# S5 input products: fp32 matmuls on four row tiles of 32 in place of split parts stacked by transfers

## The chip, the cores and the metric

One core of one Trainium2 chip runs the whole kernel. TensorE (PE in the profile, PEld its weight loads) multiplies, VectorE (DVE) and ScalarE (ACT) do elementwise work, GpSimd (POOL) some small work, SyncE (SP) issues the transfers. The metric is the device time of one execution in microseconds, as the median of several runs; lower is better.

## The reference

One decoder layer for 256 tokens of width 2048, in float32. After an RMS norm, one large projection (`w_in`) feeds three parallel branches: S5, a state-space scan; an RG-LRU scan; and stick-breaking attention. Each branch goes through its own projection and a sigmoid gate, the sum goes through `w_out`, and a squared-ReLU MLP and a last norm follow. The part that matters here is the start of the S5 branch:

```python
ug = u32.transpose(1, 0, 2).reshape(L, bsz, S5_GROUPS, S5_GROUP)      # 64 groups of 16 channels
bu = lax.complex(jnp.einsum('lbgc,gpc->lbgp', ug, jnp.real(b_bar)),   # 64 states for each group
                 jnp.einsum('lbgc,gpc->lbgp', ug, jnp.imag(b_bar)))
...
h = linear_scan(a, bu)
y = (einsum(real(h), c_re) - einsum(imag(h), c_im)) + d_skip * u32
```

Every group of 16 channels is multiplied by a small matrix B (16 x 64, a real and an imaginary part), which gives 64 complex inputs of a linear scan along the 256 tokens; C brings the scan's states back to 16 channels.

## The kernel before

**Weights.** All large weights stream in units of 256 x 512 (512 KB). For each unit SyncE issues a load into `raw` (three buffers, line 130), ScalarE rounds it to the matmul's reduced fp32 format into `hi` (line 146), VectorE subtracts to get the rest `lo` (line 147; four buffers for each of the two), and TensorE multiplies hi by hi, hi by lo and lo by hi (lines 225 to 227 with 256 columns at a time in `chunk`, 241 to 243 with 512 in `chunk_tok`, 276 to 278 in `pair_tok`). `next_unit` (line 151) keeps loads up to four and splits up to three units ahead of the unit in use.

**Side work.** Everything else is written as Python generators, whose steps end at `yield`. After each unit, `pump` (line 179) lets every running generator advance by its rate of steps per unit, and orders what they issue behind that unit's last instructions. S5 runs at 1.27 steps a unit (`S5_RATE`, line 590). The Tile framework then settles the order on each engine at compile time: it takes instructions by priority, lets one that is not ready be passed by one that is, and puts semaphores between engines and on reused buffers.

**PSUM.** It has two pools of four banks each: `psm` for the large products and `pss` (line 58, tag "ps") for all small ones: S5's input products `ps_v`, its output products `ps_y`, and attention's `ps_z`, `ps_c` and `ps_o`. A bank comes free when the last reader of its tile is done.

**S5.** The 1024 channels lie in eight blocks of 128 (`us5`, 128 x 8 x 256 in fp32). A block has eight groups of 16 channels, that is four pairs; a pair fills 32 partitions and yields 128 states (the partitions of a product), for the real and the imaginary part. Before, a block's input products were made in three stages.
- `s5_split` (lines 618 to 625): ScalarE rounds the block's channels (620), VectorE takes the rest (621); for each of the two groups of a pair ScalarE multiplies B by a mask that zeroes the other group's rows (624), and VectorE takes the rest of that (625). The results lie in `ux`.
- `s5_stack` (lines 629 to 631): for each pair `t` three transfers, issued by SyncE, put the rounded parts and the rests under each other in `stk`, so that 96 partitions hold channels hi, lo, hi against B hi, hi, lo.
- Then `s5_scan` makes, for each pair `t`, two matmuls over these 96 rows (line 654, real and imaginary part, 256 columns each) into one bank `ps_v`, and ScalarE copies the bank into `v` (line 656). A step ends after every second pair.

The split of the next block follows the copies, its transfers are issued during the first four scans. VectorE then turns `v` by the tables (lines 665 to 675), scans (line 710), turns back (lines 686 to 697); eight fp32 matmuls on four column tiles of 32 (line 703, `tile_position=(0, t * 32)`) give the block's output `ps_y`, and VectorE adds the skip term from that bank (line 705). There is no step's end between line 705 of one block and the first input products of the next, so both belong to one step.

S5 runs beside the LRU branch's gates, attention's projections and attention, and its own gates; `finish(sq)` closes it before the `w_glu` products.

Of the kernel before, what the change touches and what calls it, by code (L numbers as in the profile page):

```python
# [9 lines left out]
F32 = mybir.dt.float32  # L10
# [12 lines left out]
NG = 64  # L23
NT = 4
PAR = {"norm_mix_g": 16, "norm_mlp_g": 16, "s5_d": 8, "s5_b_glu": 8, "lru_conv_b": 8,
       "lru_lambda": 8, "lru_b_r": 8, "lru_b_i": 8, "lru_conv_w": 32, "grp_mask": 2, "steps": 16}
DFF = 8192
NH = 8
EPS = 1e-6
# [17 lines left out]
def hybrid_block(ctx: ExitStack, tc: tile.TileContext, io, out):  # L47
# [239 lines left out]
    def small(name):  # L287
        o = 0
        for n_, w_ in PAR.items():
            if n_ == name:  # L290
                return par[:, o:o + w_]
            o += w_
# [12 lines left out]
    s5 = ExitStack()  # L305
    sp = s5.enter_context(tc.tile_pool(name="s5", bufs=1))
    us5 = sp.tile([P, WT, L], F32, name="us5")
    bco = sp.tile([P, WT, 2, 64], F32, name="bco")
    ce = sp.tile([P, 2, 32, 2, 16], F32, name="ce")
    ux = sp.tile([P, 4, L], F32R, name="ux")  # L310
    rad = sp.tile([P, 32], F32, name="rad")
    fw = sp.tile([P, 2, 32], F32, name="fw")
    pp = s5.enter_context(tc.tile_pool(name="s5w", bufs=1))
# [66 lines left out]
    def v2(t):  # L380
        return t.rearrange("p (a l) -> p a l", a=2)
# [4 lines left out]

    dsk = small("s5_d")
    bgl = small("s5_b_glu")
    mask = small("grp_mask")
    steps = small("steps")  # L390

    def repeat(a, n):
# [222 lines left out]
        f = "p n a b -> p n (a b)"  # L615
        return (c.rearrange(f), s.rearrange(f)), gen()

    def s5_split(ct):
        bx = [ux[:, 2 + i, :].rearrange("p (r g s) -> p r g s", r=2, g=2) for i in range(2)]
        nc.scalar.copy(ux[:, 0, :], us5[:, ct, :])  # L620
        nc.vector.tensor_tensor(ux[:, 1, :], us5[:, ct, :], ux[:, 0, :].bitcast(F32), ALU.subtract)
        for g in range(2):
            m = mask[:, g:g + 1]
            nc.scalar.activation(bx[0][:, :, g, :], bco[:, ct], AF.Copy, scale=m)
            nc.vector.scalar_tensor_tensor(bx[1][:, :, g, :], bco[:, ct], m, bx[0][:, :, g, :].bitcast(F32), ALU.mult, ALU.subtract)

    stk = sp.tile([P, NT, 2, L], F32R, tag="stk", name="stk")[0:96]

    def s5_stack(t):
        for i, w_ in enumerate((ux[:, 0:4:2, :], ux[:, 1:3, :], ux[:, 0:4:3, :])):  # L630
            nc.sync.dma_start(stk[i * 32:i * 32 + 32, t].bitcast(F32), w_[t * 32:t * 32 + 32].bitcast(F32))

    gq = []

    def s5_scan():
        v = ypool.tile([P, 2, NT, L], F32, tag="yhi", name="s5_v")
        t12 = ypool.tile([P, 2, NT, L], F32, tag="ylo", name="s5_t")
        vr, vi, t1, t2 = v[:, 0], v[:, 1], t12[:, 0], t12[:, 1]
        tabs, more = s5_tables(0)
        yield from more  # L640
        s5_split(0)
        yield
        yield
        for t in range(NT):
            s5_stack(t)
            yield
        tt = nc.vector.tensor_tensor
        for b in range(WT):
            c, s = tabs
            t3 = pp.tile([P, NT, L], F32, tag="t3", name=f"t3_{b}")  # L650
            for t in range(NT):
                ps = pss.tile([P, CH], F32, tag="ps", name=f"ps_v{b}")
                for i in range(2):
                    nc.tensor.matmul(ps[:, i * L:(i + 1) * L], stk[:, t, 1, i * P:(i + 1) * P], stk[:, t, 0, :], start=i == 0, stop=True,
                                     skip_group_check=True)
                nc.scalar.copy(v[:, :, t, :], v2(ps))
                if t % 2:
                    yield
            more = iter(())
            if b + 1 < WT:  # L660
                s5_split(b + 1)
                tabs, more = s5_tables(b + 1)
                yield
            next(more, None)
            tt(t1, vr, c, ALU.mult)
            yield
            tt(t2, vi, s, ALU.mult)
            yield
            tt(t1, t1, t2, ALU.add)
            yield  # L670
            tt(t3, vi, c, ALU.mult)
            yield
            tt(vr, vr, s, ALU.mult)
            yield
            tt(t3, t3, vr, ALU.subtract)
            next(more, None)
            yield
            for x_ in (t1, t3):
                for t in range(NT):
                    j = b * NT + t  # L680
                    tt_scan(x_[:, t, :], rad[:, j:j + 1].broadcast_to([P, L]), x_[:, t, :])
                    if b + 1 < WT and x_ is t1:
                        s5_stack(t)
                    yield
            next(more, None)
            tt(t2, t1, c, ALU.mult)
            yield
            tt(vr, t3, s, ALU.mult)
            next(more, None)
            yield  # L690
            tt(t2, t2, vr, ALU.subtract)
            yield
            tt(vi, t3, c, ALU.mult)
            yield
            tt(t1, t1, s, ALU.mult)
            yield
            tt(t1, t1, vi, ALU.add)
            yield
            yield
            ps = pss.tile([P, CH], F32, tag="ps", name=f"ps_y{b}")  # L700
            for k, w_ in enumerate((t2, t1)):
                for t in range(NT):
                    nc.tensor.matmul(ps[t * 32:t * 32 + 32, 0:L], ce[:, k, b * NT + t, :, :], w_[:, t, :], start=k == 0, stop=k == 1,
                                     skip_group_check=True, tile_position=(0, t * 32))
            nc.vector.scalar_tensor_tensor(us5[:, b, :], us5[:, b, :], dsk[:, b:b + 1], ps[:, 0:L], ALU.mult, ALU.add)
            if b % 2:
                gq.append(later([gelu(b)], 1.0))
# [403 lines left out]
def _lay_out(inp):  # L1111
    import numpy as np

    def chan(a, n):
        return np.ascontiguousarray(np.asarray(a).reshape(n, P).T)

    def units(a):
        a = np.asarray(a)
        k, n = a.shape
        u = a.reshape(k // (P * UK), UK, P, n // CH, CH).transpose(3, 0, 2, 1, 4)  # L1120
        return np.ascontiguousarray(u).reshape(-1, P, UK, CH)

    o = {}
    x = np.asarray(inp["x"])[0]
    o["x"] = np.ascontiguousarray(x.T.reshape(KT, P, L).transpose(1, 0, 2))
    for n in ("w_in", "w_br_s5", "w_br_lru", "w_br_attn", "w_out", "w_up", "w_down"):
        o[n] = units(inp[n][0])
    o["w_glu"] = units(inp["s5_w_glu"][0])
    o["x_res"] = np.ascontiguousarray(x.reshape(2, P, D).transpose(1, 0, 2))
    o["b_gate_row"] = np.ascontiguousarray(np.asarray(inp["b_gate"][0]).reshape(1, -1))  # L1130
    o["norm_mix_g"] = chan(inp["norm_mix_g"][0], KT)
    o["norm_mlp_g"] = chan(inp["norm_mlp_g"][0], KT)
    o["final_norm_g"] = np.ascontiguousarray(np.asarray(inp["final_norm_g"]).reshape(1, D))
    for n in ("s5_d", "s5_b_glu", "lru_conv_b", "lru_lambda"):
        o[n] = chan(inp[n][0], WT)
    o["lru_b_r"] = chan(np.asarray(inp["lru_b_r"][0]).reshape(-1), WT)
    o["lru_b_i"] = chan(np.asarray(inp["lru_b_i"][0]).reshape(-1), WT)
    o["lru_conv_w"] = np.ascontiguousarray(np.asarray(inp["lru_conv_w"][0]).reshape(4, WT, P).transpose(2, 0, 1))
    for n in ("lru_w_r", "lru_w_i"):
        o[n] = np.ascontiguousarray(np.asarray(inp[n][0]).reshape(WT, 2, 64, 64).transpose(1, 2, 0, 3))  # L1140
    o["s5_lam"] = np.ascontiguousarray(np.stack([np.asarray(inp[n][0]).reshape(32, 2, 64).transpose(1, 2, 0).reshape(P, 32)
                                                 for n in ("s5_lam_re", "s5_lam_im")], axis=1))
    o["s5_log_dt"] = np.ascontiguousarray(np.asarray(inp["s5_log_dt"][0]).reshape(32, 2).T)
    o["s5_b"] = np.ascontiguousarray(np.stack([np.asarray(inp[n][0]).reshape(WT, 8, 64, 16).transpose(1, 3, 0, 2).reshape(P, WT, 64)
                                               for n in ("s5_b_re", "s5_b_im")], axis=2))
    o["s5_c"] = np.ascontiguousarray(np.stack([np.asarray(inp[n][0]).reshape(32, 2, 16, 64).transpose(1, 3, 0, 2).reshape(P, 32, 16)
                                               for n in ("s5_c_re", "s5_c_im")], axis=1))
    m = np.zeros((P, 2), np.float32)
    m[(np.arange(P) // 16) % 2 == 0, 0] = 1.0
    m[(np.arange(P) // 16) % 2 == 1, 1] = 1.0  # L1150
    o["grp_mask"] = m
    o["steps"] = np.tile(np.arange(16, dtype=np.float32), (P, 1))
    o["lru_conv_w"] = o["lru_conv_w"].reshape(P, 4 * WT)
    o["par"] = np.concatenate([o.pop(n) for n in PAR], axis=1)
    return o
# [20 lines left out]
```

## Time and profile before

| | |
|---|---|
| median of 3 runs | 1495.38 us (1493.66 to 1497.81) |
| the profiled execution's span | 1495.0 us |
| mean granted TensorE clock | 0.997 |
| TensorE busy | 1479.8 us (99%) |
| VectorE busy | 1174.3 us (79%) |
| ScalarE busy | 775.5 us (52%) |
| transfers | 292.41 MB, mean 196 GB/s |
| first and last `ps_v` matmul | 133.9 and 540.4 us |

Times in the views are microseconds from the span's start. A row of the timeline has the start, the length, the engine, the line, the operation, what it writes and reads, and the form; "x4" means that four like instructions in a row are merged, from the first one's start to the last one's end. The end of a matmul is modelled and matmuls overlap in the array, so the step from one start to the next tells what a matmul costs the engine, and its length does not. Behind a row, in brackets, stands the idle time of the engine before it and what ended it. Rows of the view of waits have the engine and what waited, what it waited for, the total, the count and the longest. Rows of the view of stretches have the stretch, its length, the busy time and count of each engine (TensorE, weight loads, VectorE, ScalarE, GpSimd), the granted clock, the share of the transfer engines and GB/s.

### The profile page before, as it was taken

What the parts mean: (1) busy time and instruction counts of PE and PEld (TensorE: products, weight loads), DVE (VectorE), ACT (ScalarE), POOL (GpSimd) and SP (SyncE); (2) the same over time, 40 slices, a digit from 0 to 9 for tenths busy, and PEclk for the clock granted to TensorE, in tenths of its full rate; (3) what the DMA queues carried; (4) which work ended last, traced back from release to release, by engine and by line L of the source; (5) the groups of instructions that cost most, each with busy time, mean ns of one, the idle gap of its engine ahead of it and who ended that gap; (6) DMA issues with size and microseconds to landing.
All of it is one profiled execution on the core that took longest, in us unless ns stands there. A gap on an engine that the chain in (4) does not pass through costs nothing.

```text
span 1495.0 us, 19909 instructions
## 1 busy us (share of the span) xinstructions
PE 1479.8 (99%) x7518; PEld 1258.0 (84%) x7518; DVE 1174.3 (79%) x1468; ACT 775.5 (52%) x916; POOL 52.9 (4%) x74
## 2 busy tenths in 40 slices
PE   9999999999999999999999999999999999999997
PEld 9998878989887878988888888888888888888886
DVE  6878988888989989789699896568754887458954
ACT  6877556565655664444455544344433444344443
POOL 1400100000000000000000000000000000000011
PEclk9999999999999999999999999999999999999999
DMA  8557676655556756666855656666666566666664
GB/s 275 187 164 217 210 212 198 184 172 180 170 179 196 223 177 217 188 194 193 273 182 185 205 186 213 196 189 193 197 195 192 190 196 195 192 191 195 189 199 136
DMA packets 89858, 292.41 MB, mean 196 GB/s; under 512 B 12834, under 2 KB 17058, under 8 KB 89634
## 3 DMA queue, kind: packets, MB, share of 16 engines
q1 hardware_dynamic: 89618, 291.07, 62.3%
q8 instruction: 59, 0.97, 0.3%
q14 instruction: 37, 0.30, 0.1%
q10 hardware_dynamic: 144, 0.07, 0.0%
HBM read 282.71 MB, written 2.10 MB: 191 GB/s over the span
## 4 chain that ended last, share of the span: by engine, by line
PE 76%; DVE 13%; DMA 4%; issue 3%; ACT 2%; POOL 0%; SPq 0%; DVEq 0%; ACTq 0%
PE mt_w_up L242 7%; PE mt_w_up L241 7%; PE mt_w_up L243 7%; DVE lo L147 5%; PE mt_w_in L241 5%; PE mt_w_in L242 5%; PE mt_w_in L243 5%; PE mp_w_down L278 4%; PE mp_w_down L276 4%; PE mp_w_down L277 4%; PE mt_w_down L242 4%; PE mt_w_down L241 4%; PE mt_w_down L243 4%; PE mm_w_in L227 3%; PE mm_w_in L226 3%
## 5 line engine op out<-in xcount | busy, mean ns | idle before, releaser
L146 ACT CAST hi<-raw 128x1024 fp32r<-128x1024 f32 (+1 forms) x521 | 545.3, 1049 | 619.9 <-PE mt_w_up L243 119.5
L147 DVE TENSOR_TENSOR lo<-raw,hi 128x1024 fp32r<-128x1024 f32 (+1 forms) x521 | 636.8, 1224 | 276.3 <-ACT hi L146 268.5
L241 PE MATMUL mt_w_in<-hi,xhi 128*128 128x512 f32 x448 | 176.4, 394 | 0.0
L242 PE MATMUL mt_w_in<-lo,xhi 128*128 128x512 f32 x448 | 174.8, 390 | 0.0
L243 PE MATMUL mt_w_in<-hi,xlo 128*128 128x512 f32 x448 | 174.7, 390 | 0.0
L241 PE MATMUL mt_w_up<-hi,hhi 128*128 128x512 f32 x448 | 174.3, 389 | 0.0
L242 PE MATMUL mt_w_up<-lo,hhi 128*128 128x512 f32 x448 | 174.3, 389 | 0.0
L243 PE MATMUL mt_w_up<-hi,hlo 128*128 128x512 f32 x448 | 174.3, 389 | 0.0
L225 PE MATMUL mm_w_in<-xhi,hi 128*128 128x256 f32 x512 | 145.6, 285 | 1.2 <-ACT hi L146 1.2
L227 PE MATMUL mm_w_in<-xhi,lo 128*128 128x256 f32 x512 | 145.1, 284 | 1.4 <-DVE lo L147 1.4
L226 PE MATMUL mm_w_in<-xlo,hi 128*128 128x256 f32 x512 | 144.7, 283 | 0.0
L733 DVE STREAM_TRANSPOSE reluT<-relu 32x256 f32<-32x256 f32 x256 | 111.5, 436 | 4.2
L242 PE MATMUL mt_w_down<-lo,hd_hi 128*128 128x512 f32 (+1 forms) x272 | 102.5, 377 | 0.0
L241 PE MATMUL mt_w_down<-hi,hd_hi 128*128 128x512 f32 (+1 forms) x272 | 102.4, 377 | 0.0
L243 PE MATMUL mt_w_down<-hi,hd_lo 128*128 128x512 f32 (+1 forms) x272 | 102.4, 376 | 0.0
L227 PEld LDWEIGHTS mm_w_in<-xhi,lo 128*128 128x128 f32 x512 | 98.0, 192 | 2.0 <-DVE lo L147 1.9
L276 PE MATMUL mp_w_down<-hi,hd_hi 128*128 128x512 f32 x256 | 99.6, 389 | 0.0
L277 PE MATMUL mp_w_down<-lo,hd_hi 128*128 128x512 f32 x256 | 99.6, 389 | 0.0
L278 PE MATMUL mp_w_down<-hi,hd_lo 128*128 128x512 f32 x256 | 99.6, 389 | 0.0
L225 PEld LDWEIGHTS mm_w_in<-xhi,hi 128*128 128x128 f32 x512 | 98.2, 192 | 1.7 <-ACT hi L146 1.6
L243 PEld LDWEIGHTS mt_w_in<-hi,xlo 128*128 128x128 f32 x448 | 84.3, 188 | 17.7
L241 PEld LDWEIGHTS mt_w_up<-hi,hhi 128*128 128x128 f32 x448 | 84.1, 188 | 17.5
(296 smaller groups left out, 2379.2 us busy)
## 6 DMA issues: line engine op xcount, KB each, us to landing
raw<-in_w_in SPq DMA_DIRECT2D x175, 512.0 KB, 4.1
raw<-in_w_up SPq DMA_DIRECT2D x128, 512.0 KB, 4.2
raw<-in_w_down SPq DMA_DIRECT2D x128, 512.0 KB, 4.2
raw<-in_w_out SPq DMA_DIRECT2D x32, 512.0 KB, 4.3
raw<-in_w_br_lru SPq DMA_DIRECT2D x16, 512.0 KB, 4.2
raw<-in_w_br_attn SPq DMA_DIRECT2D x16, 512.0 KB, 4.2
raw<-in_w_br_s SPq DMA_DIRECT2D x16, 512.0 KB, 4.2
stk<-ux SPq DMA_DIRECT2D x96, 64.0 KB, 4.0
```

Source lines behind the costliest of these rows:

```text
L146: anchor["act"] = nc.scalar.copy(h[:, k, :], r[:, k, :]).ins
L147: anchor["dve"] = nc.vector.tensor_tensor(l_[:, k, :], r[:, k, :], h[:, k, :].bitcast(F32), ALU.subtract).ins
L225: nc.tensor.matmul(o, wh[:, kk, s], xh, start=first and ct % 2 == 0, stop=False, skip_group_check=True)
L226: nc.tensor.matmul(o, wh[:, kk, s], xl, start=False, stop=False, skip_group_check=True)
L227: mm = nc.tensor.matmul(o, wl[:, kk, s], xh, start=False, stop=last and ct % 2 == 1, skip_group_check=True)
L241: nc.tensor.matmul(banks[j], xh[:, s], wh[:, a:b], start=kt == 0, stop=False)
L242: nc.tensor.matmul(banks[j], xh[:, s], wl[:, a:b], start=False, stop=False)
L243: return nc.tensor.matmul(banks[j], xl[:, s], wh[:, a:b], start=False, stop=kt == ng * UK - 1)
L276: nc.tensor.matmul(o, xh[:, s], wh[:, kk, :], start=kt == 0, stop=False)
L277: nc.tensor.matmul(o, xh[:, s], wl[:, kk, :], start=False, stop=False)
L278: mm = nc.tensor.matmul(o, xl[:, s], wh[:, kk, :], start=False, stop=kt == ng * UK - 1)
L733: nc.vector.transpose(d_[32 * a:32 * a + 32, :, :, 32 * b:32 * b + 32], s_[32 * b:32 * b + 32, :, :, 32 * a:32 * a + 32])
```

## The change

- B is laid out on the host with zeros where the other group of the pair stands: `bco` is 128 x 8 x 2 x 2 x 64 in place of 128 x 8 x 2 x 64, 1024 KB in place of 512 KB, still one load (line 407).
- `s5_split`, `s5_stack`, `ux`, `stk` and the mask are gone. `wrwi` (line 492), which shared `stk`'s place, stays.
- The input products are plain fp32 matmuls: for each pair `t` the 32 rows of `us5` as they are against the 32 rows of `bco`, on the row tile `tile_position=(t * 32, 0)`. All four pairs have a bank of their own, taken at once; the order is the real parts of pairs 0 to 3, then the imaginary parts.
- The four copies follow, with a step's end after every second one as before. Six steps ahead of the first block are gone; the steps of a block are as many as before.

```diff
-    bco = sp.tile([P, WT, 2, 64], F32, name="bco")
+    bco = sp.tile([P, WT, 2, 2, 64], F32, name="bco")
...
-    ux = sp.tile([P, 4, L], F32R, name="ux")
...
-    def s5_split(ct):
...
-    def s5_stack(t):
...
     def s5_scan():
...
         yield from more
-        s5_split(0)
-        yield
-        yield
-        for t in range(NT):
-            s5_stack(t)
-            yield
...
             t3 = pp.tile([P, NT, L], F32, tag="t3", name=f"t3_{b}")
+            ps = [pss.tile([P, CH], F32, tag="ps", name=f"ps_v{b}_{t}") for t in range(NT)]
+            for i in range(2):
+                for t in range(NT):
+                    r_ = slice(t * 32, t * 32 + 32)
+                    nc.tensor.matmul(ps[t][:, i * L:(i + 1) * L], bco[r_, b, i, :, :], us5[r_, b, :], start=i == 0, stop=True,
+                                     skip_group_check=True, tile_position=(t * 32, 0))
             for t in range(NT):
-                ps = pss.tile([P, CH], F32, tag="ps", name=f"ps_v{b}")
-                for i in range(2):
-                    nc.tensor.matmul(ps[:, i * L:(i + 1) * L], stk[:, t, 1, i * P:(i + 1) * P], stk[:, t, 0, :], start=i == 0, stop=True,
-                                     skip_group_check=True)
-                nc.scalar.copy(v[:, :, t, :], v2(ps))
+                nc.scalar.copy(v[:, :, t, :], v2(ps[t]))
                 if t % 2:
                     yield
             more = iter(())
             if b + 1 < WT:
-                s5_split(b + 1)
                 tabs, more = s5_tables(b + 1)
                 yield
...
                     tt_scan(x_[:, t, :], rad[:, j:j + 1].broadcast_to([P, L]), x_[:, t, :])
-                    if b + 1 < WT and x_ is t1:
-                        s5_stack(t)
                     yield
```

More of the change, by code (lines that the diff above doesn't have):

```diff
@@ L25 @@
 PAR = {"norm_mix_g": 16, "norm_mlp_g": 16, "s5_d": 8, "s5_b_glu": 8, "lru_conv_b": 8,
-       "lru_lambda": 8, "lru_b_r": 8, "lru_b_i": 8, "lru_conv_w": 32, "grp_mask": 2, "steps": 16}
+       "lru_lambda": 8, "lru_b_r": 8, "lru_b_i": 8, "lru_conv_w": 32, "steps": 16}
 DFF = 8192
@@ L388, in hybrid_block @@
     bgl = small("s5_b_glu")
-    mask = small("grp_mask")
     steps = small("steps")
@@ L616, in s5_tables @@
         return (c.rearrange(f), s.rearrange(f)), gen()
-    def s5_split(ct):
[L619 to L627, printed above, removed]
-    def s5_stack(t):
-        for i, w_ in enumerate((ux[:, 0:4:2, :], ux[:, 1:3, :], ux[:, 0:4:3, :])):
-            nc.sync.dma_start(stk[i * 32:i * 32 + 32, t].bitcast(F32), w_[t * 32:t * 32 + 32].bitcast(F32))
     gq = []
@@ L1143, in _lay_out @@
     o["s5_log_dt"] = np.ascontiguousarray(np.asarray(inp["s5_log_dt"][0]).reshape(32, 2).T)
-    o["s5_b"] = np.ascontiguousarray(np.stack([np.asarray(inp[n][0]).reshape(WT, 8, 64, 16).transpose(1, 3, 0, 2).reshape(P, WT, 64)
-                                               for n in ("s5_b_re", "s5_b_im")], axis=2))
+    b2 = np.zeros((8, 16, WT, 2, 2, 64), np.float32)
+    for r, n in enumerate(("s5_b_re", "s5_b_im")):
+        a = np.asarray(inp[n][0]).reshape(WT, 8, 64, 16).transpose(1, 3, 0, 2)
+        for g in range(2):
+            b2[g::2, :, :, r, g] = a[g::2]
+    o["s5_b"] = b2.reshape(P, WT, 2, 2, 64)
     o["s5_c"] = np.ascontiguousarray(np.stack([np.asarray(inp[n][0]).reshape(32, 2, 16, 64).transpose(1, 3, 0, 2).reshape(P, 32, 16)
                                                for n in ("s5_c_re", "s5_c_im")], axis=1))
[L1148 to L1151, printed above, removed]
     o["steps"] = np.tile(np.arange(16, dtype=np.float32), (P, 1))
```

## The prediction

> **What bounds the kernel now.** I read the head of the page first, then the chain that ended last, then TensorE's own waits over the whole span.
>
> ```profile
> span 1495.0 us, 19909 instructions
> PE 1479.8 (99%) x7518; PEld 1258.0 (84%) x7518; DVE 1174.3 (79%) x1468; ACT 775.5 (52%) x916; POOL 52.9 (4%) x74
> PE 76%; DVE 13%; DMA 4%; issue 3%; ACT 2%; POOL 0%; SPq 0%; DVEq 0%; ACTq 0%
> ```
>
> ```profile
> engine line waited for: us in total, times, longest us
> PE ps_y L703 <- DVE s_t L697: 1.8, 1, 1.8
> PE mm_w_in L227 <- DVE lo L147: 1.4, 2, 0.8
> PE mm_w_in L225 <- ACT hi L146: 1.2, 2, 0.7
> PE warm L327 <- POOL eps_t L336: 1.0, 1, 1.0
> PE mp_w_up L277 <- DVE lo L147: 0.8, 1, 0.8
> PE ps_v L654 <- DVE us L705: 0.6, 1, 0.6
> ```
>
> TensorE is busy for 99% of the span, and its six kinds of waits are 6.8 us together. Everything that the change takes off VectorE, ScalarE and the transfers can give back at most a part of these 6.8 us. What it does to TensorE's own stream counts in full. The profiled execution has 1495.0 us, the median of the runs is 1495.4 us; I add to the first and leave the 0.4 us, which is far below the 0.3% (4.5 us) that a measurement of this kernel can tell from no change.
>
> **What goes away.** The views of the tiles ux and stk and of the waits in the first 130 us:
>
> ```profile
> L631 SPq DMA_DIRECT2D stk<-ux x96: 559/594/1210, 122.8 to 504.7; - x96
> L624 ACT ACTIVATE ux<-bco,par x16: 388/410/432, 122.1 to 489.0; 128x128 fp32r<-128x128 f32 x16
> L625 DVE SCALAR_TENSOR_TENSOR ux<-bco,par,ux x16: 336/345/352, 126.5 to 489.4; 128x128 fp32r<-128x128 f32 x16
> L620 ACT CAST ux<-us x8: 387/416/437, 121.8 to 488.4; 128x256 fp32r<-128x256 f32 x8
> L621 DVE TENSOR_TENSOR ux<-us,ux x8: 409/418/426, 126.2 to 488.8; 128x256 fp32r<-128x256 f32 x8
> ACT hi L146 <- DMA raw<-in_w_in: 19.4, 14, 4.7
> 112.00:200.00 88.00, 86.20 (x390) 69.77 (x390) 75.23 (x87) 56.13 (x69) 7.10 (x4) 0.98 0.68 211
> ```
>
> VectorE loses 16 x 0.345 + 8 x 0.418 = 8.9 us, ScalarE 16 x 0.410 + 8 x 0.416 = 9.9 us, and SyncE's queue 96 issues of 0.594 us, 57 us. None of it is on TensorE, and in the stretch where S5 runs TensorE waits for VectorE only 1.8 us (L697) and 0.6 us (L705). So I cost the removal at nothing but those waits. Of the 1.8 us I take all as gone: before the first block's L697 there are two splits fewer (blocks 0 and 1), 2 x (0.418 + 2 x 0.345) = 2.2 us of VectorE work. The bounds are 0 and -1.8 us, and another 1.7 us below if the slow clock behind that wait goes too (its rows follow).
>
> Six of S5's steps, those of the first split and its transfers, go as well, so at 1.27 steps a unit the blocks start about 4.7 units of weights earlier. The last row above has VectorE at 75.23 of 88 us there (columns: stretch, length, then TensorE, weight loads, VectorE, ScalarE, GpSimd); it has room, and whole units are split in advance. I take nothing for it, with up to 2 us if the room isn't there when it is wanted. The padded B makes its one load, next to the weights at 34 us, 512 KB larger. At that stretch's rate (below) it is 512 KB at 274 GB/s, 1.9 us, in which the weights behind it on SyncE's queue come later. ScalarE already waits up to 4.7 us for such a weight, and the only TensorE waits for hi or lo in the early part are the 1.2 and 1.4 us, so the split in advance covers it: nothing, or up to 1.9 us where that cover is gone.
>
> ```profile
> 0.00:37.00 37.00, 34.28 (x261) 33.47 (x262) 24.01 (x37) 24.53 (x36) 6.08 (x16) 1.00 0.89 274
> 186.00:196.00 10.00, 8.21 (x44) 5.54 (x43) 6.56 (x7) 3.94 (x5) 0.00 (x0) 0.83 0.73 243
> ```
>
> **What the products cost on TensorE.** The timeline, without and with a tiled group ahead (start, length, then the instruction; the lengths overlap, so I go by starts):
>
> ```profile
> 305.96 0.40 PE L243 MATMUL mt_w_in<-hi,xlo 128*128 128x512 f32 x1
> 306.19 0.64 PE L654 MATMUL ps_v<-stk 96*128 96x256 f32 x4
> 306.67 0.60 PE L798 MATMUL ps_z<-qT,kT 128*128 128x256 f32 x2
> ...
> 300.87 0.39 PE L243 MATMUL mt_w_in<-hi,xlo 128*128 128x512 f32 x1
> 301.19 1.07 PE L703 MATMUL ps_y<-s_t,ce 128*32 128x256 f32 x16
> 302.19 0.74 PE L654 MATMUL ps_v<-stk 96*128 96x256 f32 x4
> 302.76 0.60 PE L798 MATMUL ps_z<-qT,kT 128*128 128x256 f32 x2
> 303.20 0.38 PE L799 MATMUL ps_z<-qT,kT 128*128 128x128 f32 x2
> ```
>
> Before, four products take 306.67 - 306.19 = 0.48 us, so a block's eight take 0.96 us, with no cost at either end: ps_v starts 0.23 us after the 512-column matmul ahead of it, the usual step. No row shows fp32 on row tiles. The nearest is ps_y: eight fp32 products of 256 columns on four column tiles. An fp32 product shows as two passes, so they are 16; on the whole array one pass is 0.22 us (ps_z, one product, 303.20 - 302.76 = 0.44). It starts 0.32 us after the matmul ahead (0.09 us for the change of tiling), holds TensorE 1.00 us, and the four products behind it take 0.57 in place of 0.48 us (0.09 us for the way back). The new ps_v of a block is also eight fp32 products of 256 columns, 16 passes, four tiles at a time: by this row 0.09 + 1.00 + 0.09 = 1.18 us, 0.22 more than 0.96. Right behind a ps_y, one way back and one way in fall together: 2.18 for both against 1.18 + 0.96 = 2.14 us. The first block has no ps_y ahead, the other seven do: 0.22 + 7 x 0.04 = +0.5 us. The lower end is +0.3 (just the seven), the upper is no overlap at all, a rival below.
>
> The Trainium skill, page "TensorE: Matmul & The Clock Gate", Part 3, has a measured speedup of 3.07 for four row tiles, not four. No run here shows row tiles; an estimate from that figure is 16 passes of 0.22 us over 3.07, 1.15 us where I have 1.00, and the sum would be 8 x 0.15 = 1.2 us higher.
>
> **What the change adds: a wait for a bank.** The small pool of PSUM has four buffers. Before, a block's products took one buffer at a time, two per step. Now the four tiles of a block are taken together, and in the same step ps_y of the block before still holds one until VectorE has read it (L705). So the fourth tile cannot be written before L705, in seven of the eight blocks. The trace has one instance, since there all four tiles fell into one step:
>
> ```profile
> 483.12 1.07 PE L703 MATMUL ps_y<-s_t,ce 128*32 128x256 f32 x16
> 484.12 0.97 PE L654 MATMUL ps_v<-stk 96*128 96x256 f32 x6
> 485.70 0.50 PE L654 MATMUL ps_v<-stk 96*128 96x256 f32 x2 [0.61 <-DVE us L705]
> ```
>
> ```profile
> 482.90 2.35 DVE L147 TENSOR_TENSOR lo<-raw,hi 128x1024 fp32r<-128x1024 f32 x2
> 485.17 0.47 DVE L705 SCALAR_TENSOR_TENSOR us<-us,par,ps_y 128x256 f32<-128x256 f32 x1
> ```
>
> Six passes (three tiles) ran, then TensorE stood until 485.70, 0.06 us after L705's end; L705 itself stood behind two weight splits. The distance from the shown end of ps_y to the end of L705 is the price, here 485.64 - 484.19 = 1.45 us. The first and last of the seven:
>
> ```profile
> 189.87 1.08 PE L703 MATMUL ps_y<-s_t,ce 128*32 128x256 f32 x8 [1.79 <-DVE s_t L697]
> 536.82 0.64 PE L703 MATMUL ps_y<-s_t,ce 128*32 128x256 f32 x8
> ```
>
> ```profile
> 191.02 0.48 DVE L705 SCALAR_TENSOR_TENSOR us<-us,par,ps_y 128x256 f32<-128x256 f32 x1
> 539.13 0.48 DVE L705 SCALAR_TENSOR_TENSOR us<-us,par,ps_y 128x256 f32<-128x256 f32 x1
> ```
>
> They give 0.55 and 2.15; the seven in order 0.55, 0.73, 0.54, 1.61, 0.55, 1.45, 2.15, together 7.6 us. The new order is the first products of tiles 0 to 3, then the second ones. If TensorE takes them in that order, it stands at the fourth product; the fourth tile's two products, four passes in a row and so as long as a whole group, are then still to come, and nothing of the wait is covered: each costs its distance and about 0.1 us (ps_v starts 0.07 us ahead of ps_y's shown end, and 0.06 us follow L705). That is 7.6 + 0.7 = 8.3 us. Queued behind the waiting instruction are the rest of the group and all weight matmuls after it; ScalarE's four copies and the block's first VectorE product wait too, but nothing late hangs on them, since the blocks now come 4.7 units earlier. The other way is that the compile-time order puts weight matmuls in between and the fourth tile's two products into a group of their own. Two products on one tile are four passes in a row, as long as four rounds: once more 1.18 us, 7 x 1.18 = 8.3 us. Both ways come to the same, so I take +8.3 us. The 0.6 us of the instance above is in the old time already and goes.
>
> Sum: 1495.0 + 0.5 (products) + 8.3 (bank) - 0.6 (its old instance) - 1.8 (L697) = **1501.4 us**.
>
> **A clock that drops.** Behind the 1.79 us wait at 189.87 the weight matmuls came 0.43 us apart, not 0.23, and the stretch from 186 to 196 us has a granted clock of 0.83: 10 x 0.17 = 1.7 us lost.
>
> ```profile
> 191.26 0.63 PE L241 MATMUL mt_w_in<-hi,xhi 128*128 128x512 f32 x1
> 191.69 0.63 PE L242 MATMUL mt_w_in<-lo,xhi 128*128 128x512 f32 x1
> ```
>
> Three of the bank waits (1.45, 1.61, 2.15) are near that length. I leave one such loss in the sum, as the old time has one; none makes it 1499.7, three make it 1504.8. The same page of the Trainium skill, Part 1, puts the drop behind an idle window of some 3.4 us; by that rule no bank wait would bring one, and the sum would be 1499.7. The row here, with less than 2 us, speaks against it.
>
> **The rivals.**
> - *The bank wait is hidden.* If the order at compile time holds ps_v until L705 has been, or lets ps_v take its four buffers ahead of ps_y, no tile waits. Then groups stand alone, 8 x 0.22 = +1.8 us, without 0.6 and 1.8 us, and without the slow clock, -1.7: 1495.0 + 1.8 - 4.1 = 1492.7 us; where the L697 wait and its clock stay, 1496.2. It decides when five or more of seven blocks show no wait and no separate fourth tile. For it: in three blocks before (the row at 536.82 is the second half of a ps_y) the order was already changed so that ps_v came between ps_y's halves. Against: ps_y takes its buffer first in all of them. Not slower.
> - *Row tiles don't run side by side.* The change then doesn't do what it says: 16 passes of 0.22 us in a row are 3.5 us, 3.7 with the switches, 2.7 more than 0.96, 8 x 2.7 = +22 us; the first three tiles' six passes, 1.3 us, would cover the shorter bank waits, so 1495.0 + 22 - 0.6 - 1.8, with some 2 us of bank wait left: 1517 us. For it: no row of row tiles. Against: ps_y's 16 passes in 1.00 us on column tiles.
> - *Relief wins.* VectorE is at 85% in the stretch from 112 us, and 9 us go. All waits on L697, L705 and L277 (3.2 us) and the clock (1.7) gone with products at +0.5 and no bank wait give 1490.6 us. That is the floor; it needs every gain and no cost.
>
> **How the numbers follow.** The bank case has 0.60, its own range 1497.5 (a quarter of the waits gone, no slow clock) to 1507 (three slow clocks and 2 us of start); hidden 0.26; serial 0.08; relief 0.06. Slower by over 0.3% is over 1499.9 us: three quarters of the bank case, 0.45, and the serial one, 0.53. Faster is the relief case and a little of the hidden one, 0.07. The rest, 0.40, is within. The range from 1492 to 1507 leaves out the serial and relief cases and the outermost of the bank case.
>
> **What would show it.** In the changed profile: no stk, no ux; ps_v as 32x256 in 128 passes, a group near 1.0 us (3.5 us would be the serial case); TensorE's waits with "ps_v <- DVE us L705" near 8 us in up to seven places, or six-product groups with a pair of passes per product of a lone tile 1 to 3 us later; the wait on L697 gone or short; weight matmuls 0.43 us apart at most in a few places; VectorE at 1165 and ScalarE at 766 us. The prediction is wrong if ps_v shows no wait and no split group, or if the time comes out under 1497 us with them.

## The result and the profile after

The change is slower: 1512.77 us (1511.29 to 1513.04, 4 runs) against 1495.99 us (1493.66 to 1497.81, 4 runs). The ratio is 1.0113, with a 95% interval from 1.0100 to 1.0126, so some 17 us where the prediction had 6.4. The profiled execution has a span of 1509.5 us, 14.5 more than before; a run's time lies 1.8 us above its span. Its own run was the fastest of the four: the other three have a mean granted clock of 0.994 where it has 0.996, which is some 3 us over such a span and covers the distance to the 17 us.

From the page after, the span and the busy times:

```profile
span 1509.5 us, 19806 instructions
PE 1489.3 (99%) x7582; PEld 1259.8 (83%) x7582; DVE 1168.1 (77%) x1444; ACT 777.2 (51%) x897; POOL 50.1 (3%) x74
```

VectorE is down by 6.2 us, where 8.9 were expected; ScalarE is not down at all: 777.2 us where 766 was expected. TensorE's waits over the whole span (engine and what waited, what for, total, count, longest), those that are new or grew:

```profile
PE ps_y L679 <- DVE s_t L673: 2.8, 2, 2.2
PE ps_v L632 <- DVE us L681: 1.8, 3, 1.0
PE ps_c L787 <- DVE s L781: 1.6, 1, 1.6
...
PE ps_v L632 <- ACT s_v L635: 0.4, 1, 0.4
```

Lines 632, 673, 679 and 681 are the old 654, 697, 703 and 705. The wait for the bank (L681) is there, the wait on the block's last VectorE product (L673) is not gone, and attention's `ps_c` has a wait that it did not have. The view hides a part of the bank's wait: the end of a matmul is modelled, and the modelled ends reach into the gap. By starts, in the timeline, it shows in full.

**A group alone.** The first block's products, with no `ps_y` ahead:

```profile
119.57 0.39 PE L243 MATMUL mt_w_in<-hi,xlo 128*128 128x512 f32 x1
119.88 1.15 PE L632 MATMUL ps_v<-us,bco 32*128 32x256 f32 x16
120.96 0.50 PE L241 MATMUL mt_w_in<-hi,xhi 128*128 128x512 f32 x1
121.30 0.39 PE L242 MATMUL mt_w_in<-lo,xhi 128*128 128x512 f32 x1
```

Sixteen passes hold TensorE for 120.96 - 119.88 = 1.08 us; with 0.08 for the way into the tiling (0.31 from the matmul ahead, 0.23 is usual) and 0.11 for the way out (0.34 to the next) that is 1.27 us, where 1.18 was forecast. The row tiles do run side by side.

**A group that waits.** Block 6 behind block 5's `ps_y`, on TensorE and, below, on VectorE:

```profile
482.12 0.39 PE L243 MATMUL mt_w_br_attn<-hi,ya_lo 128*128 128x512 f32 x1
482.44 1.07 PE L679 MATMUL ps_y<-s_t,ce 128*32 128x256 f32 x16
483.44 1.12 PE L632 MATMUL ps_v<-us,bco 32*128 32x256 f32 x8
485.54 1.12 PE L632 MATMUL ps_v<-us,bco 32*128 32x256 f32 x8 [0.97 <-DVE us L681]
486.60 0.50 PE L241 MATMUL mt_w_br_attn<-hi,ya_hi 128*128 128x512 f32 x1
```

```profile
482.75 2.35 DVE L147 TENSOR_TENSOR lo<-raw,hi 128x1024 fp32r<-128x1024 f32 x2
485.02 0.47 DVE L681 SCALAR_TENSOR_TENSOR us<-us,par,ps_y 128x256 f32<-128x256 f32 x1
```

Eight passes run, then TensorE stands until 485.54, right behind L681's end at 485.49, which again stood behind two weight splits. From `ps_y`'s start to the next weight matmul it is 4.16 us.

**The slow clock.** The first block's `ps_y` and what follows, and the stretch around it (stretch, length, busy times, then the granted clock):

```profile
174.95 0.70 PE L632 MATMUL ps_v<-us,bco 32*128 32x256 f32 x4
177.86 0.64 PE L679 MATMUL ps_y<-s_t,ce 128*32 128x256 f32 x8 [2.21 <-DVE s_t L673]
178.43 3.03 PE L632 MATMUL ps_v<-us,bco 32*128 32x256 f32 x12
```

```profile
174.00:188.00 14.00, 11.65 (x55) 7.41 (x54) 8.36 (x10) 5.29 (x8) 0.00 (x0) 0.76 0.56 184
```

The wait on VectorE is longer than before (2.21 against 1.79 us), and 14 x 0.24 = 3.4 us go to the clock, twice the 1.7 us of before. Bank waits in the middle of the slow stretch follow at once; e6 below, without them, loses 1.7 us here.

**Attention.** ScalarE ahead of the new `ps_c` wait, and the wait itself:

```profile
409.44 1.15 ACT L611 ACTIVATE tc<-tc,half_pi 128x1024 f32<-128x1024 f32 x1
410.61 1.28 ACT L778 ACT_TABLE_LOAD   x1
411.91 0.53 ACT L778 ACTIVATE s<-s 128x384 f32<-128x384 f32 x1
412.34 0.51 ACT L792 ACTIVATE z<-z 128x384 f32<-128x384 f32 x1
412.86 1.28 ACT L779 ACT_TABLE_LOAD   x1
414.16 0.52 ACT L779 ACTIVATE s<-s 128x384 f32<-128x384 f32 x1
...
415.88 0.67 PE L787 MATMUL ps_c<-s,tri 128*128 128x256 f32 x2 [1.65 <-DVE s L781]
```

Between the sine of S5's tables (L611) and attention's exponential (L778) ScalarE loads a function table, and another one ahead of attention's logarithm (L779), on which VectorE's L780 and L781 and then `ps_c` hang. Before the change the steps of the two fell so that ScalarE loaded tables 29 times, now 34 times, 1.28 us each: 6.4 of the 11 us that ScalarE is over its forecast.

### The profile page after: what moved, and what is told of

Its sections match the earlier page's. It is cut to its first block, busy times and chain, and to the rows that moved or that the text cites. A ratio compares the mean times of both kernels' runs of the same rounds, so it can differ in the third digit from the quotient of the medians.

```text
span 1509.5 us, 19806 instructions
## 1 busy us (share of the span) xinstructions
PE 1489.3 (99%) x7582; PEld 1259.8 (83%) x7582; DVE 1168.1 (77%) x1444; ACT 777.2 (51%) x897; POOL 50.1 (3%) x74
## 4 chain that ended last, share of the span: by engine, by line
PE 76%; DVE 12%; DMA 4%; issue 4%; ACT 3%; SPq 0%; DVEq 0%; ACTq 0%
PE mt_w_up L241 7%; PE mt_w_up L242 7%; PE mt_w_up L243 7%; DVE lo L147 5%; PE mt_w_in L241 4%; PE mp_w_down L278 4%; PE mp_w_down L276 4%; PE mp_w_down L277 4%; PE mt_w_in L243 4%; PE mt_w_in L242 4%; PE mt_w_down L242 4%; PE mt_w_down L241 4%; PE mt_w_down L243 4%; PE mm_w_in L227 4%; PE mm_w_in L225 4%
## 5 line engine op out<-in xcount | busy, mean ns | idle before, releaser
L241 PEld LDWEIGHTS mt_w_in<-hi,xhi 128*128 128x128 f32 x448 | 84.2, 188 | 18.4 <-issue 1.7
L242 PEld LDWEIGHTS mt_w_in<-lo,xhi 128*128 128x128 f32 x448 | 84.2, 188 | 18.3 <-DVE lo L147 1.4
```

Source lines behind the costliest of these rows:

```text
L241: nc.tensor.matmul(banks[j], xh[:, s], wh[:, a:b], start=kt == 0, stop=False)
L242: nc.tensor.matmul(banks[j], xh[:, s], wl[:, a:b], start=False, stop=False)
```

## The experiments

Each was timed against runs of the kernel before on the same chip. Ratios are to before, with 95% intervals; the change itself has 1.0113 (1.0100 to 1.0126). The theory: the wait for a bank costs most. The rivals: row tiles and fp32 cost it; or the S5 blocks, six steps earlier, now meet the other work badly.

**e1, a step's end between.**

```diff
             nc.vector.scalar_tensor_tensor(us5[:, b, :], us5[:, b, :], dsk[:, b:b + 1], ps[:, 0:L], ALU.mult, ALU.add)
+            yield
```

> The changed kernel with one step's end more behind the skip term of a block, so that the next block's four banks are taken a step later, when ps_y's bank has been read. Theory (the bank wait costs most of the 16.8 us): the waits of ps_v on the skip term go, the lone fourth tiles go, each group is 16 passes in one piece near 1.0 us, and the time falls by 7 to 10 us, to 1503 to 1506. Rival (fp32 on row tiles and its switches cost it): the groups stay as dear wherever they stand, the time stays within 2 us of 1512.8. Second rival (the earlier start of S5, its waits on L673 and the slow clock cost it): the time falls by at most 3 us.

1502.46 us, ratio 1.0052 (1.0039 to 1.0065): some 9 us of the loss are gone, as the theory had it. Not all of its signs came: one wait on the skip term (0.6 us) and one lone fourth tile are left. And the step moved other work: attention's `ps_c` no longer waits, and ScalarE loads 31 tables, not 34.

**e2, six empty steps.**

```diff
         yield from more
+        for _ in range(2 + NT):
+            yield
```

> The changed kernel with six empty steps in the place of those that issued the first split and transfers, so that S5 stands against the other work as it did before the change. Theory of the bank wait: the waits of ps_v stay, the time stays within 3 us of 1512.8. Rival (the shift costs it: the wait of ps_y on the block's last VectorE product with its slow clock, attention's wait on table loads): 4 to 7 us less, 1506 to 1509, with no more table loads on ScalarE than the 29 of before.

1507.17 us, ratio 1.0081 (1.0069 to 1.0094), 29 table loads and no wait of `ps_c`: 0.0032 less than the change, 4.8 us with 2.7 us of uncertainty either way. That is the rival's figure. Both causes are there, and the shift, which the prediction had costed at nothing, is no small one. The waits for banks stayed, and behind one of them the slow clock came here (a granted clock of 0.72 from 244 to 256 us).

**e3, four banks at once in the kernel before.** `stk` and the rounded parts stay; only the four tiles are taken together and the matmuls ordered as in the change.

> The kernel before with one edit: the four banks of a block are taken at once and the eight matmuls are ordered as in the change (real parts of the four pairs, then imaginary parts); splits, transfers and reduced fp32 stay. Theory (the bank wait): 6 to 9 us over before, 1502 to 1505, with TensorE's waits of ps_v on L705 at 5 us or more. Rival (row tiles or fp32): within 2 us of before. If the order at compile time fills the wait with weight matmuls, which cost nothing without a change of tiling, it may be as little as 2 us.

1497.48 us, ratio 1.0019 (1.0011 to 1.0028): 2.8 us, the small end. Its trace says why. One block's end, on TensorE:

```profile
368.49 1.07 PE L704 MATMUL ps_y<-s_t,ce 128*32 128x256 f32 x16
369.49 0.98 PE L654 MATMUL ps_v<-stk 96*128 96x256 f32 x6
370.31 0.28 PE L225 MATMUL mm_w_in<-xhi,hi 128*128 128x256 f32 x1
...
370.90 0.28 PE L227 MATMUL mm_w_in<-xhi,lo 128*128 128x256 f32 x1
371.02 0.44 PE L654 MATMUL ps_v<-stk 96*128 96x256 f32 x2
371.30 0.28 PE L225 MATMUL mm_w_in<-xhi,hi 128*128 128x256 f32 x1
```

Three tiles run, then six weight matmuls, then the fourth tile. The order that was set at compile time filled the wait in this way in four of seven blocks, and without a change of tiling that costs next to nothing: the two late products take 0.28 us where 0.24 is usual. In the change it did so in one block of seven; in the others the products of the fourth tile stay in the row, as in block 6 above, and TensorE stands. So the number of banks alone does not cost 8 us; it costs that together with the order. Why the order differs between the two kernels was not tried.

**e4, the removal alone.** The kernel before without `s5_split(b + 1)` and `s5_stack(t)` in the blocks' loop.

> The kernel before, with the splits and transfers of blocks 1 to 7 left out: all blocks multiply the first block's stacked parts, so the output is not the reference's. What the removal alone is worth. Theory (TensorE sets the time, its waits were 6.8 us): 0 to 3 us less than before, 1493 to 1496. Rival (the relief is large and the rest of the change costs that much more): 5 us less or more.

1494.51 us, ratio 0.9995 (0.9986 to 1.0003). The page has VectorE at 1168.4 us in place of 1174.3; with most of the splits and transfers away the time does not move by what can be measured. The work that the change took off the other engines was off the path.

**e5, e1 and e2 together.**

> The changed kernel with both edits: a step's end behind the skip term and six empty steps at the start. Theory (bank wait and shifted alignment add up, the products themselves cost 0.3 us a block): 10.3 us and 5 us less than the change, 1497 to 1500, some 2 to 5 us over before. Rival (row tiles or fp32 have a further cost that neither edit touches): it stays over 1501.

1498.87 us, ratio 1.0027 (1.0017 to 1.0037), within the theory. It still has 36 table loads and a `ps_c` wait: the step that each block got shifts the blocks again. So e1 and e5 are no clean measure of either cause, and e6 was made to take the bank's wait away without a shift.

**e6, a bank of its own for `ps_y`.**

```diff
-            ps = pss.tile([P, CH], F32, tag="ps", name=f"ps_y{b}")
+            ps = psm.tile([P, CH], F32, tag="mm", name=f"ps_y{b}")
```

> The changed kernel with one word different: ps_y takes its bank from the large products' pool, so ps_v's four banks are free; steps and alignment are those of the change. Theory (bank wait): the groups of a block, ps_y and ps_v, come down from 3 to 4.4 us to about 2.4 us each, the waits of ps_v on the skip term go, the time falls by 6 to 9 us to 1504 to 1507; the wait on L673 with its slow clock stays. Rival (the step that e1 added moved something else): within 3 us of the change.

1500.09 us, ratio 1.0035 (1.0022 to 1.0048); the span is 1500.5, 9.0 under the change, although this execution lost 1.7 us to the clock at its start (0.83 from 10 to 20 us) and the change's did not. The same block's end as above:

```profile
477.00 0.39 PE L243 MATMUL mt_w_br_attn<-hi,ya_lo 128*128 128x512 f32 x1
477.32 1.07 PE L679 MATMUL ps_y<-s_t,ce 128*32 128x256 f32 x16
478.32 1.15 PE L632 MATMUL ps_v<-us,bco 32*128 32x256 f32 x16
479.40 0.50 PE L241 MATMUL mt_w_br_attn<-hi,ya_hi 128*128 128x512 f32 x1
479.74 0.40 PE L242 MATMUL mt_w_br_attn<-lo,ya_hi 128*128 128x512 f32 x1
```

`ps_y` to the next weight matmul is 2.08 us, not 4.16. Taken the same way in all seven blocks, the change is 1.2, 1.2, 1.7, 0.7, 0.7, 2.1 and 0.7 us longer than e6: 8.3 us. The fifth figure is what is left of more, as e6 waits there 1.1 us longer on L673 (1.70 against 0.55 us). The stretch from 174 to 188 us has a granted clock of 0.88 here, 1.7 us lost in place of 3.4: the second slow stretch goes with the bank waits.

**e7, the same with the six steps.**

> The same with six empty steps at the start. Theory: bank wait and shift both undone, what is left is the products' own price, 8 x 0.3 = 2.4 us over before, 1496 to 1499. Rival: over 1501, a further cost of row tiles.

1497.16 us, ratio 1.0011 (1.0002 to 1.0019), 29 table loads, and in the profiled execution a granted clock of 1.00 around the first block. With both causes undone nearly all of the loss is gone. The 1.6 us that are left are near the products' own price, though the waits of `ps_y` on VectorE are others than before too (1.2 and 0.6 us).

**e8, the kernel before with one step more ahead of the first block's `ps_y`.**

```diff
             yield
             yield
+            if b == 0:
+                yield
             ps = pss.tile([P, CH], F32, tag="ps", name=f"ps_y{b}")
```

> The kernel before with one empty step more ahead of the first block's ps_y, so that VectorE's last product of that block (L697) is done when TensorE comes to it. Theory (a wait of some 2 us on TensorE also costs 1.7 us of slow clock): no slow stretch near 190 us, 2 to 3.6 us less than before, 1491 to 1493. Rival (the wait only moves to a later instruction): within 1 us of before.

1492.02 us, ratio 0.9983 (0.9974 to 0.9992). The stretch that had a clock of 0.83:

```profile
186.00:196.00 10.00, 10.00 (x60) 7.79 (x59) 8.54 (x11) 5.43 (x9) 0.00 (x0) 1.00 0.66 233
```

One empty step takes away the 1.8 us wait and the 1.7 us of slow clock behind it. A shorter wait on L697, 0.9 us, is new in a later block; no slow clock follows it. By its median this is the fastest of all kernels here.

**e9, e7 with that step.**

> The changed kernel with ps_y in the large products' pool, six empty steps at the start, and one more step ahead of the first block's ps_y: all that helped. Theory (what is left is the products' own price, 1 to 2.4 us, against the old kernel with one step more, 1492.0): 1493 to 1496, not under the old kernel with one step more. Rival (the work taken off VectorE, ScalarE and the transfers pays once nothing else is in the way): under 1491.

1493.79 us, ratio 0.9994 (0.9985 to 1.0002). No wait on a block's last product is left, and it is 0.0011 behind e8, about 1.6 us, with 0.0012 of uncertainty either way. So the price itself is not clear of noise; what shows is that the change made well is not ahead of the old products.

**e10, two row tiles at a time and six steps.** Two tiles, two banks, copies and a step's end, then the other two.

> The changed kernel with two of the four row tiles at a time, two banks in each of two steps as before the change, and six empty steps at the start; ps_y stays in the small pool. No bank is short, but a block has two groups of four rounds in place of one. Theory (a group costs by its rounds and its two changes of tiling, 1.28 us whether two or four tiles run): 8 x 1.28 = 10 us over the kernel with its own bank and six steps, 1505 to 1509. Rival (a pass costs the same wherever it runs, so that four tiles gain nothing over two): within 2 us of that kernel, 1495 to 1499.

1501.48 us, ratio 1.0045 (1.0031 to 1.0059), 0.0034 or 5.1 us over e7. Neither side had it right in size: six blocks had their second group apart, in the other two the order put both next to each other, and behind one 1.2 us wait the slow clock came once (0.83 from 538 to 548 us). The price of a single group came out as the theory says; by it the second groups are some 9 us on TensorE, and why the runs, with 2.5 us of uncertainty, show only 5.1 is not known. A group of two tiles:

```profile
133.27 0.39 PE L243 MATMUL mt_w_br_lru<-hi,ylru_lo 128*128 128x512 f32 x1
133.58 1.13 PE L635 MATMUL ps_v<-us,bco 32*128 32x256 f32 x8
134.65 0.50 PE L241 MATMUL mt_w_br_lru<-hi,ylru_hi 128*128 128x512 f32 x1
```

Eight passes on two tiles take 1.07 us, sixteen on four took 1.08.

## Why the prediction was wrong

The direction was right and the main mechanism too; the size was not: 1512.77 us lies above the upper end of the range, 1507. The runs split the 17 us in three, each with 1 to 3 us of uncertainty. From before to e7, where neither cause is at work, it is 1.6 us; the forecast had +0.5 (products) - 0.6 (the old instance) - 1.8 (L697) = -1.9. From e7 to e6, the earlier start, it is 3.6 us, where the forecast had nothing. From e6 to the change, the wait for the bank with its clock, it is 11.7 us, where the forecast had 8.3. So the step that failed in its mechanism is the earlier start, put at nothing; the others were off in size.

- **The earlier start, forecast 0 with up to 2.** This step failed. Six steps in place again are worth 4.8 us (e2) and, with the bank's wait gone, 0.0024 or 3.6 us (e6 to e7). It holds the longer L673 wait, five table loads and the 1.6 us of `ps_c`. The prediction asked only whether VectorE had room for the earlier blocks, not what they would stand beside.
- **The wait on L697, forecast -1.8.** This step failed in the change, where the wait is 2.8 us, in two places. The reason given, 2.2 us of VectorE work fewer ahead of it, is not enough: with one of those two splits left out (e4) the wait is 1.8 us as before. With all splits gone and the six steps back, the first block's wait is none in e2 and 0.6 us in e7, without a slow clock. So what sets it is above all where the step falls among the weight splits and gates on VectorE: e8 moves it by one step, takes no work off VectorE, and the first block's wait is gone.
- **Bank wait, forecast +8.3.** Measured as 8.3 us on TensorE's own starts (the change against e6). That the sums are equal is luck: by block the forecast had 0.65, 0.83, 0.64, 1.71, 0.65, 1.55 and 2.25, and the third came out at 1.7, the last at 0.7. VectorE's order there did not stay as it was: in the change the third block's skip term stands behind a weight split, and for the last one VectorE is free and waits 0.33 us for `ps_y`. By the runs, taking the wait away is worth more, 0.0078 (change to e6) and 0.0070 (e2 to e7), that is 10.5 to 12 us with 2 to 3 us of uncertainty either way: the slow clock that comes with these waits is in it.
- **One slow stretch, forecast as before.** There are two in a row, +1.7 us, and e6 has one.
- **Products, forecast +0.5.** A lone group is 1.27 against 0.96 us. Behind `ps_y`, e6's rows give 0.09 + 1.00 + 1.08 + 0.11 = 2.28 against 2.14. That is 0.31 + 7 x 0.14 = 1.3 us; e9 against e8 says 1.6, not clear of noise. Right in kind, small in size. The serial rival is out.
- **Removal at nothing.** Right (e4).

In span, by way of e6: 1.3 (products) - 0.8 (the old instance, by starts) + 1.9 (L673, 3.7 us in e6 against 1.8 before) + 1.8 (`ps_c` with its restart) + 8.3 (bank) + 1.7 (clock) = 14.2 of the 14.5 us. It was not tried which of the parts of the shift weighs most in the runs' 17 us.

The range failed for a reason of its own: it took the side effects of the shift as one term of at most 2 us, and the runs have 3.6 to 4.8 us for it. The slow clocks behind bank waits, which its upper end had, were a fair guess.

## What to carry to other kernels

Where TensorE is busy for 99%, price a change by what it does to TensorE's stream: passes, changes of tiling, and above all who must free what before an instruction in that stream can go. Taking all of a pool's buffers at once can make every other user of the pool a wait. And where side work advances by steps, a step removed shifts all that follow it; put the steps back first, then compare.

## What the runs showed of the hardware

- Four row tiles run side by side in fp32: 16 passes in 1.08 us, where 16 passes of 0.22 us one after the other would be 3.5 us. That is a factor of 3.3, or 2.8 with the changes of tiling (1.27 us). The 3.07 that the Trainium skill has ("TensorE: Matmul & The Clock Gate", Part 3) lies between the two.
- A group on row tiles takes 0.08 us more than one on column tiles. The weight loads differ, in the change's views of the two tiles (shortest, median, longest in ns):

```profile
L632 PEld LDWEIGHTS ps_v<-us,bco x128: 181/184/332, 119.9 to 540.7; 32*128 32x128 f32 x128
L679 PEld LDWEIGHTS ps_y<-s_t,ce x128: 106/109/110, 174.4 to 590.9; 128*32 128x32 f32 x128
```

  The difference is 75 ns for 96 columns. The same page of the Trainium skill gives a load's time in its section on LDWEIGHTS as the columns over 1.2, in ns, for 32 rows as for 128. The difference agrees with an estimate from it, 80 ns; the times themselves do not: 184 and 109 ns here, where the estimates are 107 and 27. That the longer loads are the 0.08 us was not tried.
- The granted clock can drop behind a wait that is shorter than the slow stretch that follows, and the length of the wait alone does not decide it. Weight matmuls then came 0.43 us apart in place of 0.23, so about half speed, and 1.7 us lost are a slow stretch of 3.4 us. A 1.8 us wait cost 1.7 us before, one of 1.2 us cost as much in e10, and 2.2 us with bank waits behind it cost 3.4; yet the 1.6 us `ps_c` wait at 414 us in the change cost none, nor did the 1.7 us wait on L673 at 422 us in e6. Part 1 of the same page of the Trainium skill has a free-running window of 3.4 us. The lost clock in multiples of 1.7 us agrees with that length; that a whole window must be idle does not agree.
